# A prefix log-sum-exp scan: six in-place tile buffers, a straight-line TensorE program and a reordered last turn

## The chip, the cores and the metric

The kernel runs on one core of a Trainium2 chip. The metric is device time in microseconds (us), from the start to the end of one execution; the profile's span is a little shorter, since it runs from the first to the last recorded instruction. The core has five engines with their own instruction streams (TensorE or PE, VectorE or DVE, ScalarE or ACT, GpSimd or POOL, SyncE or SP), which meet only at semaphores, and 16 DMA engines that move data between the large memory (HBM) and the on-chip memory (SBUF). In this kernel SP issues all loads and ACT all stores.

## What is computed

```python
B, S, D = 8, 4096, 2048            # x is float32
out[:, 0, :] = x[:, 0, :]
for t in range(1, S):
    mx = np.maximum(out[:, t-1, :], x[:, t, :])
    out[:, t, :] = mx + np.log(np.exp(out[:, t-1, :] - mx) + np.exp(x[:, t, :] - mx))
```

This is a running log-sum-exp along S: out[t] is the logarithm of the sum of exp(x[0..t]), for each batch and each of the 2048 columns. The kernel computes it as Exp, prefix sum, Ln.

## The kernel before

Each batch's 4096 rows are cut into 8 blocks of 512 rows. A tile is one block: 128 partitions with R = 4 consecutive rows each, by D = 2048 columns, 4 MB of float32. There are NT = 64 tiles, n = 0 to 63, and each passes through the same steps, in two halves h of 1024 columns:

- SP loads tile n into an input buffer `ti` (L113 to L125). There are NI = 4 of them.
- ACT takes Exp in place (`exp`, L133).
- DVE adds the four rows within each partition, one running sum of three additions for each half (`local`, L248).
- PE multiplies each partition's last row by a strict triangle of ones (`triangle`, L224), so that every partition gets the sum of all partitions ahead of it. This goes on top of what `carry` (L213) left in the same PSUM bank for the tile before: the running total up to there.
- DVE adds that to all four rows (`join`, L257). After it, `carry` of this tile may read the joined last row for the next tile. At a batch's last block there is no carry, only a semaphore step.
- ACT takes Ln (`ln`, L140) from `ti` into one of NO = 2 output buffers `to`, and issues the store from it (L165).

A column half's semaphore chain is: exps, chain, sums, ahead, joined, carried, logs. ACT's order is written out: Exp of both halves of tile n, Ln of both halves of tile n - 1, the store of n - 1. So a tile's Ln comes behind the Exp of the next tile, and that waits for the next tile's load. The Ln's first half also waits until the store that last used its output buffer has landed (`take(act, stored[n % NO], 16)`, L139). When both Ln are done ACT raises `freed` (L164), for which SP waits before it loads into that input buffer again (L123).

All engines run loops: SP and ACT one turn per four tiles, DVE the same, PE one turn per batch of eight tiles (L233). ACT's last four tiles stand behind its loop. There the Ln is in place, in `ti`, and the store goes out from `ti` (L177). The last turn, n = 63, is ordered Ln half 0 of 62, Exp half 0 of 63, Ln half 1 of 62, the whole store of 62, Exp half 1 of 63; then Ln and store of 63, half by half.

Of the kernel before, what the change touches and what calls it, by code (L numbers as in the profile page):

```python
# [9 lines left out]
def kernel(  # L10
# [15 lines left out]

    nc = tc.nc
    f32 = mybir.dt.float32
    ACT = mybir.ActivationFunctionType
    nc.scalar.preload_act_table_set("natural_log_exp_and_others")  # L34

    B, S, D = x.shape
    P = 128
    R = 4
    NBLK = S // (P * R)
    NT = B * NBLK  # L40
    FD = 512
    NI, NO = 4, 2
    HALF = D // 2
    assert NBLK % NI == 0 and NI % NO == 0 and D == 4 * FD

    pool = ctx.enter_context(tc.tile_pool(name="io", bufs=1))
    psum = ctx.enter_context(tc.tile_pool(name="ps", bufs=1, space=bass.MemoryType.PSUM))
    before = pool.tile([P, P], f32, name="before", tag="before")
    last = pool.tile([P, P], f32, name="last", tag="last")
    ti = [pool.tile([P, R, D], f32, name=f"ti{i}", tag=f"ti{i}") for i in range(NI)]  # L50
    to = [pool.tile([P, R, D], f32, name=f"to{i}", tag=f"to{i}") for i in range(NO)]
    ps = [psum.tile([P, D], f32, name=f"ps{i}", tag=f"ps{i}") for i in range(2)]

    x_v = x.rearrange("b (k p r) d -> (b k) p r d", p=P, r=R)
# [2 lines left out]
    def half(h):  # L57
        return slice(h * HALF, (h + 1) * HALF)
# [17 lines left out]
    def take(engine, s, n):  # L76

        event(engine, [(s, n)], [(s, "sem-sub-imm", n)])

    with tc.tile_critical():  # L80
        def sems(name, n):
            return [nc.alloc_semaphore(f"{name}{i}") for i in range(n)]

        ones, shaped, freed, logs, top, final = (
            sems(s, 1)[0] for s in ("ones", "shaped", "freed", "logs", "top", "final")
        )

        loaded, stored = sems("loaded", NI), sems("stored", NO)
        exps, chain, sums, ahead, joined, carried = (
            sems(s, 2) for s in ("exps", "chain", "sums", "ahead", "joined", "carried")  # L90
        )
# [1 line left out]
        with nc.Block() as block:  # L93
# [17 lines left out]
            @block.sync  # L111
            def _(sp):
                def load(src, n):  # L113
                    sp.dma_start(out=ti[n][:], in_=src).then_inc(loaded[n], 16)


                sp.dma_start(out=ti[0][:, 0:2, :], in_=x_v[0][:, 0:2, :]).then_inc(top, 16)
                sp.dma_start(out=ti[0][:, 2:R, :], in_=x_v[0][:, 2:R, :]).then_inc(loaded[0], 16)
                for n in range(1, NI):
                    load(x_v[n], n)  # L120
                with sp.Fori(1, NT // NI) as j:
                    for n in range(NI):
                        sp.wait_ge(freed, n + 1)  # L123
                        load(x_v[bass.ds(j * NI + n, 1)][0], n)
                    take(sp, freed, NI)  # L125

            @block.scalar
            def _(act):
                def exp(n, h, rows=slice(0, R)):
                    t = ti[n % NI]  # L130
                    if h == 0:
                        take(act, loaded[n % NI], 16)
                    act.activation(  # L133
                        t[:, rows, half(h)], t[:, rows, half(h)], ACT.Exp
                    ).then_inc(exps[h], 1)

                def ln(n, h, turn, in_place=False):
                    if h == 0 and not in_place:
                        take(act, stored[n % NO], 16)  # L139
                    act.activation(  # L140
                        (ti[n % NI] if in_place else to[n % NO])[:, :, half(h)],
                        ti[n % NI][:, :, half(h)], ACT.Ln,
                    )._wait_ge(carried[h], turn + 1).then_inc(logs, 1)

                def settle(turns):
                    take(act, carried[0], turns)
                    take(act, carried[1], turns)
                    take(act, logs, 2 * turns)

                for n in range(NO):  # L150
                    act.sem_inc(stored[n], 16)
                take(act, top, 16)
                act.activation(ti[0][:, 0:2, :], ti[0][:, 0:2, :], ACT.Exp)  # L153
                exp(0, 0, slice(2, R))
                exp(0, 1, slice(2, R))
                turns = (NT - 2) // NI
                with act.Fori(0, turns) as j:
                    for n in range(1, NI + 1):
                        exp(n, 0)
                        exp(n, 1)  # L160
                        ln(n - 1, 0, n - 1)
                        ln(n - 1, 1, n - 1)

                        event(act, [(logs, 2 * n)], [(freed, "sem-add-imm", 1)])  # L164
                        act.dma_start(  # L165
                            out=o_v[bass.ds(j * NI + (n - 1), 1)][0], in_=to[(n - 1) % NO][:]
                        ).then_inc(stored[(n - 1) % NO], 16)
                    settle(NI)


                first = turns * NI
                finals = 0

                def store(n, h=None):
                    cols = slice(0, D) if h is None else half(h)
                    act.wait_ge(logs, 2 * (n - first) + (2 if h is None else h + 1))
                    act.dma_start(  # L177
                        out=o_v[n][:, :, cols], in_=ti[n % NI][:, :, cols]
                    ).then_inc(final, 16)
                    return 1  # L180

                for n in range(first + 1, NT):
                    up = n - 1
                    if n < NT - 1:
                        exp(n, 0)
                        exp(n, 1)
                        ln(up, 0, up - first, True)
                        ln(up, 1, up - first, True)
                        finals += store(up)
                    else:  # L190
                        ln(up, 0, up - first, True)
                        exp(n, 0)
                        ln(up, 1, up - first, True)
                        finals += store(up)
                        exp(n, 1)
                for h in range(2):
                    ln(NT - 1, h, NT - 1 - first, True)
                    finals += store(NT - 1, h)
                settle(NT - first)
                for n in range(NO):  # L200
                    take(act, stored[n], 16)
                take(act, final, 16 * finals)

            @block.tensor
            def _(pe):
                def carry(k, h):

                    if k == NBLK - 1:
                        event(pe, [(joined[h], k + 1)], [(carried[h], "sem-add-imm", 1)])
                        return  # L210
                    for c in range(2 * h, 2 * h + 2):
                        sl = slice(c * FD, (c + 1) * FD)
                        m = pe.matmul(  # L213
                            ps[(k + 1) % 2][:, sl], last[:], ti[k % NI][:, R - 1, sl],
                            start=True, stop=False, skip_group_check=True,
                        )
                        if c == 2 * h:
                            m._wait_ge(joined[h], k + 1)
                    m.then_inc(carried[h], 1)

                def triangle(k, h):
                    for c in range(2 * h, 2 * h + 2):
                        sl = slice(c * FD, (c + 1) * FD)
                        m = pe.matmul(  # L224
                            ps[k % 2][:, sl], before[:], ti[k % NI][:, R - 1, sl],
                            start=k == 0, stop=True, skip_group_check=True,
                        )
                        if c == 2 * h:
                            m._wait_ge(sums[h], k + 1)
                    m.then_inc(ahead[h], 1)  # L230

                pe.wait_ge(shaped, 2)
                with pe.Fori(0, B):  # L233
                    for k in range(NBLK):
                        for h in range(2):
                            triangle(k, h)
                        for h in range(2):
                            carry(k, h)
                    for h in range(2):
                        take(pe, sums[h], NBLK)  # L240
                        take(pe, joined[h], NBLK)

            @block.vector
            def _(dve):
# [14 lines left out]
                        ps[n % 2][:, half(h)].unsqueeze(1).to_broadcast([P, R, HALF]),  # L259
                    )._wait_ge(ahead[h], n + 1).then_inc(joined[h], 1)  # L260

                with dve.Fori(0, NT // NI):
                    for n in range(NI):
                        for h in range(2):
                            local(n, h)
                        for h in range(2):
                            join(n, h)
                    for h in range(2):
                        take(dve, exps[h], NI)
                        take(dve, chain[h], (R - 2) * NI)  # L270
                        take(dve, ahead[h], NI)


# [28 lines left out]
```

The softmax here doesn't subtract the row's maximum and nothing guards it: scores larger than these inputs give would overflow.

## Time and profile before

| | |
|---|---|
| time, median of 5 runs | 1254.31 us (1254.03 to 1257.6) |
| profiled execution | 1254.35 us, span 1252.6 us |
| moved | 268.44 MB read, 268.44 MB written, mean 429 GB/s |
| loads, 4096 KB each | x63, median 33.9 us from issue to landing |
| stores from `to`, 4096 KB each | x60, median 31.4 us |
| stores from `ti` in the last turns | x3 of 4096 KB, median 22.4 us; x2 of 2048 KB, median 7.4 us |
| Exp, one half (L133) | mean 3582 ns, x128 |
| Ln, one half (L140) | mean 3609 ns into `to`, x120; mean 3606 ns in place, x8 |
| row additions (L248), join (L257) | mean 1224 ns, x384; mean 4417 ns, x128 |
| matmuls (L224, L213) | x512 and x448, and as many weight loads |

How to read it: a load or store is far longer from issue to landing than its data needs on the wire, because loads and stores wait behind each other in two queues, one for SP's and one for ACT's. The page gives for each of 40 equal slices of the span the mean busy share of the 16 DMA engines in tenths and the GB/s. Each transfer is split over all 16 DMA engines and counts as landed when the last of them is done. The trace records those 16 completions one by one, and each DMA packet with its queue, start, duration and size. A window view sums the busy time of the engines, the DMA share and the rate for chosen stretches of time, counted from the span's start.

### The profile page before, as it was taken

The page shows a single profiled execution, that of the slowest core. Times are in us where ns is not written, and L with a number is a line of the kernel's source. Part 1 is how long each engine was busy: PE and PEld are TensorE (multiplying, and loading weights), DVE is VectorE, ACT ScalarE, POOL GpSimd, SP SyncE. Part 2 cuts the span into 40 slices and gives each one's busy share as a digit, 9 for nine tenths or more (in the row PEclk, how much of TensorE's full clock was granted, in tenths as well). Part 3 has the DMA queues.
Part 4 walks back from the last instruction along what each step waited for, and adds up shares of the span by engine and source line. Part 5 has one row for each costly group of instructions (what it writes and reads, how often), then busy time and mean ns, then how long its engine had stood idle before and what let it go on. Part 6 is the DMA issues. An engine that isn't in the chain of part 4 may idle for free. (4 is left out here: it accounts for less than half of the span.)

```text
span 1252.6 us, 3677 instructions
## 1 busy us (share of the span) xinstructions
PE 644.1 (51%) x960; PEld 212.4 (17%) x960; DVE 1022.9 (82%) x512; ACT 913.2 (73%) x258; POOL 1.1 (0%) x8
## 2 busy tenths in 40 slices
PE   2556355463554646546455554455645555346552
PEld 0121011121111211112112111111111211111110
DVE  4999788797887877878778788787887878878784
ACT  5886776777767668677686776867768668676884
POOL 0000000000000000000000000000000000000000
PEclk9988677876878867788687786877868877688785
DMA  9999999999999999999999999999999999999997
GB/s 402 419 435 435 430 431 432 431 434 435 435 435 431 430 432 432 433 435 435 435 432 429 433 431 434 434 435 435 432 431 431 431 434 435 434 435 433 429 433 300
DMA packets 19490, 536.90 MB, mean 429 GB/s; under 512 B 2080, under 2 KB 2080, under 8 KB 3104
## 3 DMA queue, kind: packets, MB, share of 16 engines
q1 hardware_dynamic: 9360, 268.44, 49.8%
q10 hardware_dynamic: 10128, 268.44, 49.7%
q8 instruction: 1, 0.02, 0.0%
q14 instruction: 1, 0.01, 0.0%
HBM read 268.44 MB, written 268.44 MB: 429 GB/s over the span
## 5 line engine op out<-in xcount | busy, mean ns | idle before, releaser
L248 DVE TENSOR_TENSOR ti<-ti 128x1024 f32<-128x1024 f32 x384 | 464.7, 1224 | 207.7 <-ACT ti L133 198.9
L140 ACT ACTIVATE to<-ti 128x4096 f32<-128x4096 f32 x120 | 427.6, 3609 | 248.6 <-ACTq L62 244.8
L257 DVE TENSOR_TENSOR ti<-ti,ps 128x4096 f32<-128x4096 f32 x128 | 560.1, 4417 | 9.0 <-PE ps L224 8.7
L224 PE MATMUL ps<-ti,before 128*128 128x512 f32 x512 | 374.7, 882 | 355.1 <-DVE ti L248 354.6
L133 ACT ACTIVATE ti<-ti 128x4096 f32<-128x4096 f32 (+1 forms) x128 | 452.6, 3582 | 59.8 <-ACTq L62 59.4
L213 PE MATMUL ps<-ti,last 128*128 128x512 f32 x448 | 269.6, 732 | 235.5 <-DVE ti L257 235.5
L224 PEld LDWEIGHTS ps<-ti,before 128*128 128x128 f32 x512 | 127.0, 275 | 618.2 <-DVE ti L248 512.9
L213 PEld LDWEIGHTS ps<-ti,last 128*128 128x128 f32 x448 | 85.4, 211 | 402.6 <-DVE ti L257 337.5
L140 ACT ACTIVATE ti<-ti 128x4096 f32<-128x4096 f32 x8 | 28.7, 3606 | 14.5 <-PEq L62 8.9
L153 ACT ACTIVATE ti<-ti 128x4096 f32<-128x4096 f32 x1 | 3.6, 3616 | 6.4 <-ACTq L62 6.4
L34 ACT ACT_TABLE_LOAD x1 | 1.3, 1283 | 0.8 <-PEq L286 0.8
L101 POOL TENSOR_SCALAR_AFFINE_SELECT before<-before 128x128 f32<-128x128 f32 x1 | 0.3, 294 | 0.1
L106 POOL TENSOR_SCALAR_AFFINE_SELECT last<-last 128x128 f32<-128x128 f32 x1 | 0.3, 294 | 0.0
L97 POOL MEMSET before<- 128x128 f32 x1 | 0.2, 205 | 0.5 <-SPq L80 0.5
L98 POOL MEMSET last<- 128x128 f32 x1 | 0.2, 205 | 0.0
L286 POOL MEMSET const-bfloat16-1.0<- 128x1 bf16 x1 | 0.1, 102 | 0.0
L286 POOL MEMSET const-uint8-127<- 128x1 uint8 x1 | 0.1, 102 | 0.0
L286 POOL MEMSET const-float32-0.0<- 128x1 f32 x1 | 0.1, 99 | 0.3 <-issue 0.3
L286 POOL MEMSET const-float32-1.0<- 128x1 f32 x1 | 0.1, 99 | 0.0
## 6 DMA issues: line engine op xcount, KB each, us to landing
ti<-in_x_dram SPq DMA_DIRECT2D x63, 4096.0 KB, 33.9
out_dram<-to ACTq DMA_DIRECT2D x60, 4096.0 KB, 31.4
out_dram<-ti ACTq DMA_DIRECT2D x3, 4096.0 KB, 22.4
ti<-in_x_dram SPq DMA_DIRECT2D x2, 2048.0 KB, 9.6
out_dram<-ti ACTq DMA_DIRECT2D x2, 2048.0 KB, 7.4
```

The lines of the kernel that those rows point to most:

```text
L34: nc.scalar.preload_act_table_set("natural_log_exp_and_others")
L97: g.memset(before[:], 1.0).then_inc(ones, 1)
L101: g.affine_select(out=before[:], in_=before[:], compare_op=mybir.AluOpType.is_ge, fill=0.0, base=-1, pattern=[[1, P]], channel_multiplier= ...
L106: g.affine_select(out=last[:], in_=last[:], compare_op=mybir.AluOpType.is_ge, fill=0.0, base=-(P - 1), pattern=[[0, P]], channel_multiplier=1,
L133: act.activation(t[:, rows, half(h)], t[:, rows, half(h)], ACT.Exp).then_inc(exps[h], 1)
L140: act.activation((ti[n % NI] if in_place else to[n % NO])[:, :, half(h)], ti[n % NI][:, :, half(h)], ACT.Ln,)._wait_ge(carried[h], turn + ...
L153: act.activation(ti[0][:, 0:2, :], ti[0][:, 0:2, :], ACT.Exp)
L213: m = pe.matmul(ps[(k + 1) % 2][:, sl], last[:], ti[k % NI][:, R - 1, sl], start=True, stop=False, skip_group_check=True,)
L224: m = pe.matmul(ps[k % 2][:, sl], before[:], ti[k % NI][:, R - 1, sl], start=k == 0, stop=True, skip_group_check=True,)
L248: a = dve.tensor_add(t[:, r, half(h)], t[:, r - 1, half(h)], t[:, r, half(h)])
L257: dve.tensor_add(t[:, :, half(h)], t[:, :, half(h)], ps[n % 2][:, half(h)].unsqueeze(1).to_broadcast([P, R, HALF]),)._wait_ge(ahead[h], n ...
L286: nc = _bacc.Bacc("TRN2", target_bir_lowering=False, num_devices=1)
```

## The change

- The two output buffers go; there are six buffers `ti`, and Ln is in place for all tiles. Load, Exp, sums, Ln and store of a tile use the same buffer.
- SP waits before a new load for the landing of the store from that buffer (one `stored` semaphore per buffer) instead of for the Ln. The semaphore `freed`, the ScalarE step that raised it and the Ln's wait for an output buffer go. SP also takes the last landings at the end, instead of ACT.
- The loops of SP, ACT and DVE have six tiles per turn, with the remaining four tiles behind them.
- PE has no loop: all 64 tiles are written out, and its semaphores `sums` and `joined` count up to 64.
- The last turn is ordered Exp half 0 of 63, Ln half 0 of 62, store of that half, Exp half 1 of 63, Ln half 1 of 62, store of that half; then Ln and store of 63 by halves, as before.

```diff
-    NI, NO = 4, 2
+    NI = 6
-    to = [pool.tile([P, R, D], f32, name=f"to{i}", tag=f"to{i}") for i in range(NO)]
...
-                with sp.Fori(1, NT // NI) as j:
+                turns = (NT - NI) // NI
+                with sp.Fori(1, turns + 1) as j:
                     for n in range(NI):
-                        sp.wait_ge(freed, n + 1)
+                        take(sp, stored[n], 16)
                         load(x_v[bass.ds(j * NI + n, 1)][0], n)
-                    take(sp, freed, NI)
+                for n in range((turns + 1) * NI, NT):
+                    take(sp, stored[n % NI], 16)
+                    load(x_v[n], n % NI)
+                for n in range(NT - NI, NT):
+                    take(sp, stored[n % NI], 32 if n >= NT - 2 else 16)
...
-                def ln(n, h, turn, in_place=False):
-                    if h == 0 and not in_place:
-                        take(act, stored[n % NO], 16)
+                def ln(n, h, turn):
+                    t = ti[n % NI]
                     act.activation(
-                        (ti[n % NI] if in_place else to[n % NO])[:, :, half(h)],
-                        ti[n % NI][:, :, half(h)], ACT.Ln,
+                        t[:, :, half(h)], t[:, :, half(h)], ACT.Ln
                     )._wait_ge(carried[h], turn + 1).then_inc(logs, 1)
+
+                def store(n, dst, turn, h=None):
+                    cols = slice(0, D) if h is None else half(h)
+                    act.wait_ge(logs, 2 * turn + (2 if h is None else h + 1))
+                    act.dma_start(
+                        out=dst[:, :, cols], in_=ti[n % NI][:, :, cols]
+                    ).then_inc(stored[n % NI], 16)
...
-                        event(act, [(logs, 2 * n)], [(freed, "sem-add-imm", 1)])
-                        act.dma_start(
-                            out=o_v[bass.ds(j * NI + (n - 1), 1)][0], in_=to[(n - 1) % NO][:]
-                        ).then_inc(stored[(n - 1) % NO], 16)
+                        store(n - 1, o_v[bass.ds(j * NI + (n - 1), 1)][0], n - 1)
...
                 for n in range(first + 1, NT):
-                    up = n - 1
+                    up, turn = n - 1, n - 1 - first
+                    exp(n, 0)
                     if n < NT - 1:
-                        exp(n, 0)
                         exp(n, 1)
-                        ln(up, 0, up - first, True)
-                        ln(up, 1, up - first, True)
-                        finals += store(up)
-                    else:
-                        ln(up, 0, up - first, True)
-                        exp(n, 0)
-                        ln(up, 1, up - first, True)
-                        finals += store(up)
+                    ln(up, 0, turn)
+                    if n == NT - 1:
+                        store(up, o_v[up], turn, 0)
                         exp(n, 1)
+                    ln(up, 1, turn)
+                    store(up, o_v[up], turn, 1 if n == NT - 1 else None)
...
-                with pe.Fori(0, B):
-                    for k in range(NBLK):
-                        for h in range(2):
-                            triangle(k, h)
-                        for h in range(2):
-                            carry(k, h)
+                for n in range(NT):
                     for h in range(2):
-                        take(pe, sums[h], NBLK)
-                        take(pe, joined[h], NBLK)
+                        triangle(n, h)
+                    for h in range(2):
+                        carry(n, h)
+                for h in range(2):
+                    take(pe, sums[h], NT)
+                    take(pe, joined[h], NT)
...
-                with dve.Fori(0, NT // NI):
-                    for n in range(NI):
+                def turn(tiles):
+                    for n in range(tiles):
...
+                with dve.Fori(0, NT // NI):
+                    turn(NI)
+                turn(NT % NI)
```

More of the change, by code (lines that the diff above doesn't have):

```diff
@@ L41 @@
     FD = 512
-    NI, NO = 4, 2
+    NI = 6
     HALF = D // 2
-    assert NBLK % NI == 0 and NI % NO == 0 and D == 4 * FD
+    assert NI % 2 == 0 and NBLK % 2 == 0 and D == 4 * FD
     pool = ctx.enter_context(tc.tile_pool(name="io", bufs=1))
@@ L82, in sems @@
             return [nc.alloc_semaphore(f"{name}{i}") for i in range(n)]
-        ones, shaped, freed, logs, top, final = (
-            sems(s, 1)[0] for s in ("ones", "shaped", "freed", "logs", "top", "final")
+        ones, shaped, logs, top = (
+            sems(s, 1)[0] for s in ("ones", "shaped", "logs", "top")
         )
-        loaded, stored = sems("loaded", NI), sems("stored", NO)
+        loaded, stored = sems("loaded", NI), sems("stored", NI)
         exps, chain, sums, ahead, joined, carried = (
@@ L148, in settle @@
                     take(act, logs, 2 * turns)
-                for n in range(NO):
-                    act.sem_inc(stored[n], 16)
                 take(act, top, 16)
@@ L162, in _ @@
                         ln(n - 1, 1, n - 1)
-                        event(act, [(logs, 2 * n)], [(freed, "sem-add-imm", 1)])
-                        act.dma_start(
-                            out=o_v[bass.ds(j * NI + (n - 1), 1)][0], in_=to[(n - 1) % NO][:]
-                        ).then_inc(stored[(n - 1) % NO], 16)
+                        store(n - 1, o_v[bass.ds(j * NI + (n - 1), 1)][0], n - 1)
                     settle(NI)
                 first = turns * NI
-                finals = 0
@@ L174, in store @@
[L174 to L180, printed above, removed]
                 for n in range(first + 1, NT):
-                    up = n - 1
+                    up, turn = n - 1, n - 1 - first
@@ L195, in _ @@
+                    if n == NT - 1:
+                        store(up, o_v[up], turn, 0)
                         exp(n, 1)
+                    ln(up, 1, turn)
+                    store(up, o_v[up], turn, 1 if n == NT - 1 else None)
                 for h in range(2):
-                    ln(NT - 1, h, NT - 1 - first, True)
-                    finals += store(NT - 1, h)
+                    ln(NT - 1, h, NT - 1 - first)
+                    store(NT - 1, o_v[NT - 1], NT - 1 - first, h)
                 settle(NT - first)
-                for n in range(NO):
-                    take(act, stored[n], 16)
@@ L202, in _, with carry @@
-                take(act, final, 16 * finals)
             @block.tensor
             def _(pe):
-                def carry(k, h):
-                    if k == NBLK - 1:
-                        event(pe, [(joined[h], k + 1)], [(carried[h], "sem-add-imm", 1)])
+                def carry(n, h):
+                    if n % NBLK == NBLK - 1:
+                        event(pe, [(joined[h], n + 1)], [(carried[h], "sem-add-imm", 1)])
                         return
@@ L213, in carry @@
                         m = pe.matmul(
-                            ps[(k + 1) % 2][:, sl], last[:], ti[k % NI][:, R - 1, sl],
+                            ps[(n + 1) % 2][:, sl], last[:], ti[n % NI][:, R - 1, sl],
                             start=True, stop=False, skip_group_check=True,
@@ L217, in carry, with triangle @@
                         if c == 2 * h:
-                            m._wait_ge(joined[h], k + 1)
+                            m._wait_ge(joined[h], n + 1)
                     m.then_inc(carried[h], 1)
-                def triangle(k, h):
+                def triangle(n, h):
                     for c in range(2 * h, 2 * h + 2):
@@ L224, in triangle @@
                         m = pe.matmul(
-                            ps[k % 2][:, sl], before[:], ti[k % NI][:, R - 1, sl],
-                            start=k == 0, stop=True, skip_group_check=True,
+                            ps[n % 2][:, sl], before[:], ti[n % NI][:, R - 1, sl],
+                            start=n % NBLK == 0, stop=True, skip_group_check=True,
                         )
                         if c == 2 * h:
-                            m._wait_ge(sums[h], k + 1)
+                            m._wait_ge(sums[h], n + 1)
                     m.then_inc(ahead[h], 1)
                 pe.wait_ge(shaped, 2)
-                with pe.Fori(0, B):
-                    for k in range(NBLK):
-                        for h in range(2):
-                            triangle(k, h)
-                        for h in range(2):
-                            carry(k, h)
-                    for h in range(2):
-                        take(pe, sums[h], NBLK)
-                        take(pe, joined[h], NBLK)
+                for n in range(NT):
+                    for h in range(2):
+                        triangle(n, h)
[4 more added lines that the diff above has]
+                    take(pe, joined[h], NT)
             @block.vector
@@ L268, in _ @@
                     for h in range(2):
-                        take(dve, exps[h], NI)
-                        take(dve, chain[h], (R - 2) * NI)
-                        take(dve, ahead[h], NI)
+                        take(dve, exps[h], tiles)
+                        take(dve, chain[h], (R - 2) * tiles)
+                        take(dve, ahead[h], tiles)
+                with dve.Fori(0, NT // NI):
+                    turn(NI)
+                turn(NT % NI)
 _INS = ['x']
```

## The prediction

> **What bounds the kernel now.** I read the DMA rows of the page first. The kernel moves 268.44 MB in and 268.44 MB out.
>
> ```profile
> PE 644.1 (51%) x960; PEld 212.4 (17%) x960; DVE 1022.9 (82%) x512; ACT 913.2 (73%) x258; POOL 1.1 (0%) x8
> ...
> DMA  9999999999999999999999999999999999999997
> GB/s 402 419 435 435 430 431 432 431 434 435 435 435 431 430 432 432 433 435 435 435 432 429 433 431 434 434 435 435 432 431 431 431 434 435 434 435 433 429 433 300
> ```
>
> Every slice but the last has all 16 DMA engines busy, and no compute engine is above 82%. Then the waits:
>
> ```profile
> ACT to L140 <- ACTq L62: 244.8, 57, 5.6
> ```
>
> This Ln wait, 4.3 us for each of 57 tiles, is ScalarE idle under a full DMA. So time can be won or lost only where a DMA engine is idle, or gets other work. The stage view of the end:
>
> ```profile
> 1205.70:1211.20 5.50, 3.15 (x7) 1.17 (x8) 5.50 (x2) 1.24 (x1) 0.00 (x0) 0.99 1.01 435
> 1211.20:1223.00 11.80, 5.07 (x6) 1.17 (x4) 6.17 (x4) 10.47 (x3) 0.00 (x0) 0.64 1.02 442
> 1223.00:1234.10 11.10, 6.86 (x8) 2.35 (x8) 7.24 (x5) 3.77 (x2) 0.00 (x0) 0.50 0.90 387
> 1234.10:1239.20 5.10, 0.70 (x1) 0.00 (x0) 5.10 (x2) 3.62 (x1) 0.00 (x0) 0.83 0.05 19
> 1239.20:1240.30 1.10, 0.00 (x0) 0.00 (x0) 0.43 (x1) 0.55 (x1) 0.00 (x0) 0.50 0.00 0
> 1240.30:1251.20 10.90, 0.00 (x0) 0.00 (x0) 0.00 (x0) 3.07 (x1) 0.00 (x0) 0.50 0.97 385
> ```
>
> The last two columns are DMA share and GB/s. From 1234.1 to 1239.2 the rate is 19 GB/s, 97 KB in all: three packets of 32 KB. One engine is finishing tile 62's store alone; from 1239.2 to 1240.3 nothing moves.
>
> The landing records show this engine directly: a transfer completes in 16 increments, one for each DMA engine, each with its time. Load 63 lands from 1205.7 to 1211.1. Fourteen engines finish within 0.9 us of the first, one 1.63 us after it, one 5.4 us. Following these two back through all transfers:
> - The 5.4 us engine ("slow") falls behind evenly, 0.09 us in each 19.36 us that a tile takes.
> - The 1.63 us engine ("fetch") keeps time until 107 us, then is suddenly later and stays so. There the queue table's instruction packet went:
>
> ```profile
> q1 hardware_dynamic: 9360, 268.44, 49.8%
> q10 hardware_dynamic: 10128, 268.44, 49.7%
> q8 instruction: 1, 0.02, 0.0%
> ```
>
> The packet records give q8's packet 16,384 bytes and 936 ns from 106.87. On that engine the next packet but one starts at 109.40, where the 1,210 ns rhythm before it pointed to 108.08: 1.32 us lost for one fetch.
>
> The end's compute chain:
>
> ```profile
> 1239.07 0.62 ACTq L177 DMA_DIRECT2D out_dram<-ti  x1
> 1239.75 3.62 ACT L140 ACTIVATE ti<-ti 128x4096 f32<-128x4096 f32 x1 [0.71 <-PEq L62]
> 1243.40 0.54 ACTq L177 DMA_DIRECT2D out_dram<-ti  x1
> ```
>
> Tile 63's half stores are issued at 1239.07 and 1243.40 and land 7.0 and 7.8 us later, the last at 1251.2. The span ends 1.4 us after that, and the execution's 1254.35 is 1.75 more; the median of the runs, 1254.31, is the same within 0.04.
>
> **What the Trainium skill says.** "DMA: Bandwidth & Descriptors", § Where 436 GB/s comes from, puts the ceiling of one core at 435 GB/s; the trace's best slices agree (435). Its § Latency and other measured facts says that two of the 16 engines are usually slower; one here is. Its § Queues, rings and completion order says that each DMA engine serves its own ring of each queue, round robin by packet; the records agree, load and store packets alternating. "Runtime: NRT & Kernel Launch", § Instruction fetch mechanics, says that a sequencer streams its program through its own DMA queue in blocks of 16 KiB, 256 instructions, "mostly hidden". The 16,384-byte packet agrees in size; hidden from the sequencer it is, from a saturated DMA engine it isn't.
>
> **The change, part by part.**
>
> *Six buffers in place.* The same 24 MB is now one pool. A buffer is held from its load's issue to its store's landing. Tiles pass every 19.36 us, so six give 6 x 19.36 = 116 us per buffer. Needed: load and store at half the bandwidth each (2 x 19.4), and between them a wait for the next tile's load, its two Exp and this tile's two Ln (19.4 + 4 x 3.6 = 34): 73 us. The 43 left stand as queued transfers. Neither queue runs dry; if that cover were gone, each missing us would count once per six tiles. The Ln's wait on an output buffer goes (244.8 us of idle ScalarE): what is late next is the load, so nothing comes of it. SP now waits for a store's landing instead of the Ln's end; behind it stand only later loads, which the bigger pool covers. At the start six loads are queued instead of four, but store 0 and load 4 already follow load 3 without a gap (load 3's first landing 43.98, then 16 packets to load 4's at 63.35): 0. VectorE's and ScalarE's new loop lengths: same instructions, hidden: 0.
>
> *The last turn.* The 14 quick engines finish store 61 at 1223.87 and have no idle time before it. Then come tiles 62 and 63, now four half stores. Back to back one takes 5.12 us (first landings of the two in before, 1245.87 and 1250.99): 20.5, so 1244.35. Is the data there? Tile 63's chain from its load's landing, with the rows' durations: Exp 3.7, Ln of 62 with its issue 4.0, Exp 3.6, three adds 3.7, joins 4.4 and 4.4, Ln 3.6, so half stores at about 23 and 28 us. A quick engine has 39 us of stores left when it finishes load 63, less what the latest engine's lag delays the chain. Any engine that is itself late has its full 39 and no gap. So the idle 6 us of the quick engines goes. But the slow engine idled only 1.4 us (1239.1 to about 1240.5): it would end near 1244.35 + 5.5 = 1249.9, against 1251.2. That is the gain, 1.3 us, if nothing else comes.
>
> *Straight-line TensorE program.* 960 weight loads, 960 matmuls and about 20 more are now about 1,940 instructions, each passed once. The loop before has a 1/8 of them and was fetched once at its first pass. The fetch at 107 us came after about 185 instructions. One more each 256 gives 185, 441, 697, 953, 1209, 1465, 1721: seven fetches instead of one (six or eight if the last block is counted otherwise). The records of before show one per queue, so not whether all come through one DMA engine. Bounds: 0, where each finds another engine; 7 x 1.32 = 9.25 where all go to one. I take one, because a ring belongs to a queue and an engine. Then the fetch engine ends at 1244.35 + 0.31 (its place before 107 us) + 9.25 = 1253.9. A TensorE stall while a block arrives would be hidden: its work has the 43 us above.
>
> *The sum.* Last landing 1253.9 instead of 1251.2, +2.7 us: 1254.35 + 2.7 = 1257.0.
>
> **The rivals.**
> 1. *The fetches cost nothing on the path* (spread over engines). The slow engine ends last, 1249.9: -1.3, 1253.0, not slower. For: "mostly hidden"; a later 8 KB fetch, near 1183 us, fell on a third engine, 0.68 us late. Against: that one is of another queue (q14), and the first one was not hidden from its engine. It decides at four fetches or fewer on one engine: 0.31 + 4 x 1.32 = 5.6, the slow engine's lag.
> 2. *And the slow engine isn't slow any more*, its drift being an effect of the loops. All 16 end at about 1244.9: -6.3, 1248.0, faster. For: the drift has no named cause in the trace. Against: it is even through all loop turns.
> 3. *The fetches fall on the slow engine.* 5.5 + 9.25 = 14.8 behind: last landing 1259.1, +7.9, 1262.3. Against: in before it was another one.
> 4. *In-place buffers starve the loads.* By the 43 us above, excluded unless compute stalls by that much.
>
> **How the numbers follow.** 0.2% is 2.5 us, about what a measurement here can tell from no change; the edge is 1256.8. Forecast 0.56, with its own range 1255.6 (six fetches) to 1258.5 (eight); rival 1 0.22; rival 2 0.11; rival 3 0.09; rival 4 0.02. The forecast's centre lies just beyond the edge, so it gives 0.34 to slower and 0.22 to no change. Faster: rival 2 and a little of rival 1, 0.13. Same 0.42. Slower 0.45. The range takes in rival 1 and the forecast, 1252.0 to 1260.0.
>
> **What would show it.** q8 with seven packets, about 0.11 MB; one DMA engine losing 1.3 us about every 155 us; load 63's landing spread near 9.6 us instead of 5.4; no zero-rate stretch on that engine in the last turn; the rate falling to one engine's for the last several us; ScalarE's Ln waiting for no store. One q8 packet only, a spread of 5.4, or a q8 landing on changing engines would make it wrong; so would a row of slices under 430 GB/s in the middle, which would mean starved queues.

## The result and the profile after

The changed kernel takes 1250.88 us (median), the kernel before 1254.32: a ratio of 0.9967, 95% interval 0.996 to 0.9974. The forecast was 1257.0, slower; it is faster by 3.4 us. The profiled execution took 1250.61 us, span 1248.9. All ratios compare mean times and leave out slow executions, over 1.5% above the fastest of their kernel: here one of the changed kernel's 27 (1276.74), below two of e6's six.

The page of the changed kernel, the rows that were read first before:

```profile
span 1248.9 us, 3456 instructions
...
PE 653.6 (52%) x960; PEld 216.0 (17%) x960; DVE 1023.3 (82%) x512; ACT 907.2 (73%) x258; POOL 1.1 (0%) x8
...
DMA  9999999999999999999999999999999999999998
GB/s 403 420 436 428 431 435 436 430 433 432 435 435 429 435 430 436 436 428 435 431 436 435 429 436 431 435 436 429 436 430 436 436 428 436 431 435 435 429 436 357
...
q1 hardware_dynamic: 9360, 268.44, 49.9%
q10 hardware_dynamic: 11040, 268.44, 49.9%
q8 instruction: 7, 0.11, 0.0%
```

Little changed in the middle: full DMA, and compute times within 2% of those before. The last slice moved 357 GB/s instead of 300. And q8 has seven packets: the count of instruction fetches came as forecast. The end in stages (us, then busy time of PE, PEld, DVE, ACT and POOL, the TensorE clock, DMA share and GB/s):

```profile
1223.00:1234.10 11.10, 3.78 (x4) 1.17 (x4) 9.27 (x3) 5.66 (x3) 0.00 (x0) 0.50 0.96 397
1234.10:1239.20 5.10, 0.00 (x0) 0.00 (x0) 0.00 (x0) 1.91 (x1) 0.00 (x0) 0.50 1.03 422
1239.20:1240.30 1.10, 0.00 (x0) 0.00 (x0) 0.00 (x0) 0.00 (x0) 0.00 (x0) 0.50 1.02 417
1240.30:1251.20 10.90, 0.00 (x0) 0.00 (x0) 0.00 (x0) 0.00 (x0) 0.00 (x0) 0.51 0.39 162
```

Where before moved 19 and 0 GB/s, from 1234.1 to 1240.3, all DMA engines now work, and the low rate has moved to the very end, where single engines finish. Who makes them late is in the landing records, read as in the prediction: 16 completions for each transfer. Here they are for four loads, worked out from the trace: first the time at which the first engine is done, then the lag of each of the 16 behind it, in us, sorted:

```
 139.5  0.0 0.0 0.0 0.0 0.1 0.1 0.2 0.5 0.5 0.5 0.5 0.5 0.5 0.6 0.6 2.1
 488.0  0.0 0.0 0.0 0.0 0.1 0.1 0.5 0.5 0.5 0.5 0.5 0.5 1.6 1.8 2.0 2.0
 836.6  0.0 0.0 0.0 0.0 0.1 0.1 0.5 0.5 0.5 0.5 1.8 1.8 1.9 1.9 2.0 2.6
1185.1  0.0 0.0 0.1 0.5 0.5 0.5 0.5 1.0 1.4 1.5 1.8 1.8 1.8 1.9 2.0 3.8
```

Each fetch moves one more engine by about 1.3 us, and never the same one: at the end seven engines stand between 1.4 and 2.0, none at 9.6. The last number of the last row, 3.8, is the slow engine, whose lag grows evenly from load to load; no fetch hit it. It lands the last store at 1247.5, again 3.8 us behind the first. The forecast had the fetch engine at 1253.9.

The waits show a second difference. In the view of who waited for whom (in total, times, longest), the wait ahead of Exp before and now:

```profile
ACT ti L133 <- ACTq L62: 59.4, 63, 6.0
...
ACT ti L136 <- ACTq L59: 304.1, 63, 6.0
```

Before, ScalarE waited 244.8 us ahead of Ln and 59.4 ahead of Exp, together 304.2. Now it waits 304.1 ahead of Exp and for no store ahead of Ln. The idle time hasn't shrunk, it stands at another place in each tile.

### The profile page after: what moved, and what is told of

Same layout as the page of the kernel before. It is cut to its first block, busy times and chain, and to the rows that moved or that the text cites. A ratio compares the mean times of both kernels' runs of the same rounds, so it can differ in the third digit from the quotient of the medians.

```text
span 1248.9 us, 3456 instructions
## 1 busy us (share of the span) xinstructions
PE 653.6 (52%) x960; PEld 216.0 (17%) x960; DVE 1023.3 (82%) x512; ACT 907.2 (73%) x258; POOL 1.1 (0%) x8
## 5 line engine op out<-in xcount | busy, mean ns | idle before, releaser
L136 ACT ACTIVATE ti<-ti 128x4096 f32<-128x4096 f32 (+1 forms) x128 | 452.6, 3582 | 310.1 <-ACTq L59 304.1
L208 PE MATMUL ps<-ti,before 128*128 128x512 f32 x512 | 379.9, 894 | 339.5 <-DVE ti L232 338.9
L142 ACT ACTIVATE ti<-ti 128x4096 f32<-128x4096 f32 x128 | 455.4, 3602 | 11.5 <-PE ps L197 6.0
L197 PE MATMUL ps<-ti,last 128*128 128x512 f32 x448 | 273.9, 743 | 234.3 <-DVE ti L241 234.3
L159 ACT ACTIVATE ti<-ti 128x4096 f32<-128x4096 f32 x1 | 3.6, 3616 | 6.5 <-ACTq L59 6.5
## 6 DMA issues: line engine op xcount, KB each, us to landing
ti<-in_x_dram SPq DMA_DIRECT2D x63, 4096.0 KB, 38.4
out_dram<-ti ACTq DMA_DIRECT2D x62, 4096.0 KB, 43.9
```

Of the source, the lines that this page charges most:

```text
L136: act.activation(t[:, rows, half(h)], t[:, rows, half(h)], ACT.Exp).then_inc(exps[h], 1)
L142: act.activation(t[:, :, half(h)], t[:, :, half(h)], ACT.Ln)._wait_ge(carried[h], turn + 1).then_inc(logs, 1)
L197: m = pe.matmul(ps[(n + 1) % 2][:, sl], last[:], ti[n % NI][:, R - 1, sl], start=True, stop=False, skip_group_check=True,)
L208: m = pe.matmul(ps[n % 2][:, sl], before[:], ti[n % NI][:, R - 1, sl], start=n % NBLK == 0, stop=True, skip_group_check=True,)
```

## Experiments

Ratios are to the kernel before, from runs on the same chip, with the 95% interval in brackets. Since they compare means, one long execution moves them more than it moves the median.

### The kernel before, again (e1)

No edit.

> The kernel before, unchanged, for the lag of the slow DMA engine. If the smaller lag in the changed kernel (3.9 us behind the first engine at the end, 5.5 in the profile before) is chance from run to run, this profile gives some other value, anywhere from 3 to 6 us. If the lag belongs to the kernel, it is again 5.3 to 5.7 us at load 63. Time 1253.5 to 1255 either way.

Measured: 1253.88 us, ratio 1.0003 (0.9994 to 1.0012). In its profile the slow engine is 4.4 us behind at the store of tile 61, the last one ahead of the gap; in the profile on record it was 5.5. So this lag isn't a fixed property of the kernel, and the 5.5 that the prediction carried over is the highest of the six profiles in which Ln waits for a store.

### The last turn alone (e2)

```diff
                 for n in range(first + 1, NT):
                     up = n - 1
+                    exp(n, 0)
                     if n < NT - 1:
-                        exp(n, 0)
                         exp(n, 1)
...
+                    ln(up, 0, up - first, True)
+                    if n == NT - 1:
+                        finals += store(up, 0)
+                        exp(n, 1)
+                    ln(up, 1, up - first, True)
+                    finals += store(up, 1 if n == NT - 1 else None)
```

> The kernel before with only the last turn reordered and tile 62 stored by halves. If the last turn is the whole gain: 3.4 us faster, 1250.9. If it is only the slow engine's idle time (2.2 us lost between the stores of 62 and 63 in the profile before) and the rest comes from the smaller lag of that engine in the changed kernel: 2.0 us faster, about 1252.3.

Measured: 1251.89 us, 0.9983 (0.9977 to 0.999): 2.2 us less than before. The stage in which before moved 19 GB/s:

```profile
1234.10:1239.20 5.10, 0.00 (x0) 0.00 (x0) 0.00 (x0) 2.83 (x1) 0.00 (x0) 0.50 1.03 413
```

The gap is gone: on its own, the new order is enough to close it.

### The straight-line TensorE program alone (e3)

In the kernel before, the loop of L233 becomes `for n in range(NT)`, as in the change.

> The kernel before with only the TensorE program written out. Seven instruction packets. If each falls on another DMA engine: no change, 1254.3 within 0.5 us, and the landing spread of load 63 stays that of the slow engine. If they piled up on one engine, as the prediction had it: its lag 9.6 us at load 63, and since this kernel's last turn waits for that landing, 4 us slower, 1258.5. If leaving out the loop is what makes the slow engine less slow: lag 3.8 instead of 5.4, and 1.6 us faster, 1252.7.

Measured: 1254.11 us, 1.0004 (0.9996 to 1.0011), seven q8 packets, the slow engine 4.5 us behind at tile 61's store. Within that interval, about 1 us either way, seven fetches cost nothing and leaving out the loop brings nothing. This is the term on which the forecast's sign stood.

### The change without its last turn (e4)

The changed kernel with Ln half 0 of 62 ahead of Exp half 0 of 63 again, and tile 62 stored whole.

> The changed kernel with the last turn in the order of before and tile 62 stored whole. If the last turn is the whole gain: back at 1254.3. If the gain is split between it and the smaller lag: 2.0 us slower than the changed kernel, about 1252.9.

Measured: 1250.75 us, 0.9978 (0.9967 to 0.9989). Neither expectation: without the new last turn the changed kernel is as fast as with it. Its end on ScalarE (start, duration, then what it is and the idle time ahead of it):

```profile
1208.13 3.62 ACT L142 ACTIVATE ti<-ti 128x4096 f32<-128x4096 f32 x1 [3.53 <-PE ps L200]
1211.65 3.60 ACT L136 ACTIVATE ti<-ti 128x4096 f32<-128x4096 f32 x1
...
1234.67 0.63 ACTq L149 DMA_DIRECT2D out_dram<-ti  x1
```

The order is that of before, but all of it is 4.4 us earlier: the Ln at 1208.13 stood at 1212.53, and the store of tile 63's first half was issued at 1239.07. The slow engine finishes tile 62 at 1237.8, and now its next data is there. (One execution of 1255.11 among seven raises the ratio.) So something in the six in-place buffers and their waits brings the tail forward, a second way to close the same gap.

### Both, with two separate output buffers (e5)

The kernel before with e2's last turn and e3's TensorE program.

> The kernel before with the new last turn and the straight-line TensorE program, but with the two separate output buffers. The last turn alone gave 1251.9, the changed kernel gives 1250.9. If the missing 1 us comes with the six in-place buffers: 1251.9 again. If it comes with the missing TensorE loop: 1250.9.

Measured: 1251.55 us, 0.9972 (0.9961 to 0.9982). The interval overlaps those of the changed kernel and of e2. The median lies nearer to e2's, but the median of before beside it was 0.5 us higher too (1254.58 against 1254.05). It doesn't decide.

### Which wait it is (e11, e12)

e11 takes e4 and puts back one thing: Ln of tile n waits for the store of tile n - 2. SP counts the landings in a semaphore of its own (`take` waits for a count and subtracts it).

```diff
                         take(sp, stored[n], 16)
+                        sp.sem_inc(landed, 1)
...
+                act.sem_inc(landed, 2)
...
+                        take(act, landed, 1)
                         ln(n - 1, 0, n - 1)
```

> The changed kernel with the last turn of before (1250.75 without the following) and one wait put back: the first Ln of tile n waits, as before, until the store of tile n - 2 has landed. If this wait is what made the kernel before late in its last turn, by holding back the Exp of the next tile: Exp of tile 63 late again by about 4 us, the gap between the stores of 62 and 63 is back, and the time is 1253 to 1254. If the in-place buffers close the gap in another way: 1250.8.

Measured: 1253.94 us, 0.9991 (0.9977 to 1.0006): the whole gain is gone. The gap is back, at the same 19 GB/s as before:

```profile
1234.10:1239.20 5.10, 0.23 (x1) 0.00 (x0) 5.10 (x2) 3.62 (x1) 0.00 (x0) 0.82 0.05 19
```

and so is the late Ln of tile 62:

```profile
1212.30 3.62 ACT L144 ACTIVATE ti<-ti 128x4096 f32<-128x4096 f32 x1 [5.98 <-PE ps L204]
```

e12 is the same program with `act.sem_inc(landed, 4)`, so that the wait asks for a store that has long landed; the two counts left over are taken at the end.

> The kernel with the wait put back (1253.94), with the same instructions, but the wait asks for the store of tile n - 4 instead of n - 2, so that it is always met. If holding the Ln back is what costs: back at 1250.8, no gap between the last stores, and the slow engine 3.9 to 4.3 us behind at the store of tile 61, as in the four profiles without that wait (4.4 to 5.5 in the six with it). If the 120 more semaphore instructions themselves slow that engine: its lag stays at 4.8, and about 1251.5.

Measured: 1250.94 us, 0.997 (0.9957 to 0.9983). The instructions are the same but for the two counts at the end, nothing waits, and the gain is there: 3.0 us between the medians of e11 and e12, on two chips whose medians for the kernel before agree (1254.22 and 1254.28). Tile 62's Ln starts 2.8 us earlier than in e11:

```profile
1209.49 3.62 ACT L144 ACTIVATE ti<-ti 128x4096 f32<-128x4096 f32 x1 [3.36 <-PE ps L205]
```

This profile is of the longest of e12's nine executions (1254.86), with the slow engine 8.3 us behind, so it doesn't decide between the two lags that were expected. But the gap can be told apart from the lag. Here, worked out from the landings, are the lag of the last engine at tile 61's store, the time at which that store has landed, the last landing of all, and what lies between the two (us):

```
before           5.5   1229.4   1251.2   21.8
e11              4.9   1228.7   1251.0   22.3
e12              8.3   1232.0   1251.6   19.6
e4               4.1   1228.0   1247.6   19.6
e2               4.8   1228.7   1248.5   19.7
changed kernel   3.9   1227.7   1247.5   19.8
```

With the gap the last two tiles' stores take 21.8 to 24.0 us (before, e1, e3, e11), without it 19.6 to 19.8 (the other four above, and e5, e7, e8, e9). So e12's long execution is one whose slow engine came late to tile 61. An engine that finishes tile 62 only at 1241.7, as there, would have found its next data in e11's order too (issued at 1238.84), so the gain is shown by e12's other eight executions, 1250.80 to 1251.34 us against 1252.68 to 1255.25 in e11, and by the earlier Ln.

How the wait works is seen a few tiles ahead of the end. The timeline of before, at tile 61 (the Ln is that of tile 59, the Exp that of 61):

```profile
1169.89 7.13 ACT L140 ACTIVATE to<-ti 128x4096 f32<-128x4096 f32 x2 [4.50 <-ACTq L62]
1177.26 0.35 ACTq L165 DMA_DIRECT2D out_dram<-to  x1
1178.14 7.12 ACT L133 ACTIVATE ti<-ti 128x4096 f32<-128x4096 f32 x2 [1.12 <-ACTq L62]
```

and of the changed kernel, tile 61's Exp and tile 60's Ln:

```profile
1169.52 7.12 ACT L136 ACTIVATE ti<-ti 128x4096 f32<-128x4096 f32 x2 [5.29 <-ACTq L59]
1176.55 7.11 ACT L142 ACTIVATE ti<-ti 128x4096 f32<-128x4096 f32 x2
1183.69 0.35 ACTq L149 DMA_DIRECT2D out_dram<-ti  x1
```

Before, load 61 had landed at 1172.2, but ScalarE was held in front of Ln until tile 57's store had landed, and came to the Exp only at 1178.14, 5.9 us after its data. In the changed kernel the load lands at 1169.4 and the Exp starts 0.1 us later. In the middle of the run these 6 us cost nothing, since the DMA queues are full. At the end nothing refills them: VectorE runs back to back from tile 61 on (16.2 us a tile), and 4.4 us of the lateness are left at tile 62's Ln.

### The other parts (e7, e8)

e7: the changed kernel with tile 62 stored whole after both its Ln.

> The changed kernel with tile 62 stored whole after both its Ln, instead of by halves. If the slow engine's continuous work sets the end: two half stores took 9.9 us on it, a whole one 9.7, so 0.2 us faster, 1250.7. If the early half store is needed to keep that engine busy: slower by the idle time it would fill, 1 us or more.

Measured: 1250.79 us, 0.9961 (0.9946 to 0.9977). The half stores are neither needed nor dear. e8 puts one line ahead of loads 4 and 5:

```diff
                 for n in range(1, NI):
+                    if n >= 4:
+                        sp.wait_ge(logs, 2 * (n - 3))
                     load(x_v[n], n)
```

> The changed kernel, but loads 4 and 5 are issued only when Ln of tiles 0 and 1 are done, as in the kernel before, instead of at the start. If the six loads queued up front are what makes the DMA engines start more evenly (the spread of the first landings after 40 us is 0.4 us in the changed kernel, 0.5 to 1.9 us with four loads): about 0.9 us slower, 1251.8. If not: 1250.9.

Measured: 1251.01 us, 0.9963 (0.995 to 0.9977). The longer queue at the start brings nothing.

### How far fetches can be driven (e6, e9, e10)

e6 adds `for _ in range(128): pe.wait_ge(shaped, 2)` to each tile's TensorE program.

> The changed kernel with 128 more TensorE instructions per tile, waits on a semaphore that is already raised, so that about 39 blocks are fetched instead of 7. If the fetches go round the 16 DMA engines and each costs its engine 1.32 us, the slow engine gets two or three of them: 2.6 to 4.0 us slower than the changed kernel, 1253.5 to 1254.9. If a fetch costs nothing when DMA engines are full[...]: 1250.9. If all went through one engine: 39 x 1.32 = 51 us, about 1298.

Measured: 1286.06 us, with six executions between 1278.98 and 1302.66, and 1.0217 (1.0182 to 1.0252). There are 23 q8 packets, not 39, since the waits went two to an instruction: 7,552 instructions against 3,456. The profile is of one of the two longest executions (1301.68), so only these counts are taken from it. The loss over the changed kernel, about 31 us by the two ratios, is some ten times what the price of a fetch gives, so either a fetch has another cost or the waits do. e9 adds instructions that are no waits: every matmul is cut into four of 128 columns.

```diff
-                    for c in range(2 * h, 2 * h + 2):
-                        sl = slice(c * FD, (c + 1) * FD)
+                    for c in range(8 * h, 8 * h + 8):
+                        sl = slice(c * FD // 4, (c + 1) * FD // 4)
```

What the pieces leave in PSUM isn't what the whole matmuls leave, so the prefix sums are not those of the reference; transfers and waits are as described, and VectorE and ScalarE are as busy as in the changed kernel (1023.2 and 907.2 us).

> The changed kernel with every matmul cut into four of 128 columns: the same sums, about 7,700 TensorE instructions instead of 1,940, about 30 fetches instead of 7. If fetches go round the DMA engines at 1.32 us each, every engine gets about two: 2.6 us slower than the changed kernel, 1253.5. If instead the 35 us of the kernel with many waits came from the fetches in some other way, they come again here: 1280 or more. If the slow engine gets none: 1250.9.

Measured: 1257.63 us, 1.0018 (1.0004 to 1.0032), some 6.4 us more than the changed kernel by the two ratios. The queue row:

```profile
q8 instruction: 30, 0.49, 0.1%
```

Thirty fetches, and no 31 us: what e6 lost wasn't the fetches. The lags of the DMA engines in the profile of e9 (an execution of 1255.89 us), for three loads:

```
 720.6  0.0 0.1 0.4 0.7 0.7 0.9 1.1 2.7 2.8 3.0 3.4 3.5 3.9 4.2 5.7 6.5
 953.0  0.0 0.1 0.4 0.7 0.7 0.8 1.1 3.5 4.1 4.2 4.2 4.7 5.2 5.5 5.6 8.1
1146.6  0.0 0.1 0.4 0.7 0.7 0.9 1.1 4.0 4.7 4.8 5.5 5.6 5.6 6.6 7.0 9.5
```

Seven engines don't move at all between 720 and 1147 us. The last one, the slow engine, rises evenly, 0.27 us per 38.7 us, without a step. The eight between them rise in steps of 1.3 us: from the first row to the last, with eleven fetches between, together from 29.2 us behind to 43.8, 1.33 us for each fetch. So the fetches go round eight of the 16 engines, and the slow one isn't among them in this run. That it drifts twice as fast here as in the changed kernel (9.3 us behind at tile 61's store, not 3.9) is what costs the time of this execution, since from there to the last landing both take 19.8 us. Why it drifts faster was not found.

e10 puts e6's waits into a small loop, to execute them with few fetches.

> The changed kernel with the same 128 additional waits per tile on TensorE, but in a small loop, so that some 10 to 12 blocks are fetched instead of 23. If executing the waits is what stretched the DMA packets and cost 35 us: 1280 or more again. If the fetches did: about 1251 to 1252.

Measured: 1461.92 us, 1.1649 (1.1601 to 1.1697), ten q8 packets. The view of waits says why it can't answer the question:

```profile
PEld ps L208 <- issue: 774.9, 445, 17.9
...
DVE ti L244 <- PE ps L208: 401.8, 64, 7.2
```

TensorE's own instruction stream is now the bound (774.9 us in which its weight loads waited for nothing but issue), VectorE waits for it, and the time is that of another kernel.

## Why the prediction was wrong

- **DMA as the bound, the idle gap at 1234 to 1240 us, 1.32 us for a fetch, seven fetches:** all held. Seven packets came, and e9 confirms the price (1.33).
- **"I take one, because a ring belongs to a queue and an engine":** this step failed, and with it the sign. The fetches fall on different DMA engines, so each engine loses 1.3 us once, below the slow engine's lag, and the path loses nothing (e3: 1.0004). Of the two bounds written down, 0 and 9.25 us, the lower was right. That is rival 1, at 1253.0; one packet in the trace before could not tell the two apart. The Trainium skill's "DMA: Bandwidth & Descriptors", § Queues, rings and completion order, gives a queue one ring on each of 16 engines; that a queue's fetches stay on one of them was an inference of mine, not its statement. Its "Runtime: NRT & Kernel Launch", § Instruction fetch mechanics, has the fetch "mostly hidden", and for seven of them e3 agrees.
- **"The Ln's wait on an output buffer goes ... so nothing comes of it":** this failed too, the other way. It is worth 3.0 us with the old last turn (e11 against e12), nearly all of the gain. The working looked at the share of idle time, which indeed doesn't change, and not at where in a tile it stands. Moved from in front of Ln to in front of Exp, it lets each tile start when its load lands, and in the last tiles that is 4.4 us.
- **The last turn, -1.3 us:** right in direction and too small when it stands alone (e2: -2.2), but wrong in the sum: the removed wait closes the same gap, so on top of it the new order brings nothing (e4 against the changed kernel). Two edits that fill one gap were costed as if only one did.
- **Sizes:** rival 1 was still 2.1 us too slow. Its quick engines end at 1243.7 instead of 1244.35, since a half store that follows another takes 4.97 us there, not 5.12 as the pair of before; why it takes less, no run shows. Its slow engine is 3.8 us behind instead of 5.5. Together that is 2.3 us at the last landing.
- **Loads, start, loop lengths, buffers held longer: 0.** Held: e8 shows it for the start. From issue to landing loads now take 38.4 us and stores of whole tiles 43.9 (medians); less the 2 x 19.4 of their own, 43.5 us are spent queued, where 43 were worked out as cover.

What stays open is the lag of the slow engine. The medians of e2 and e5 are 1.0 and 0.7 us above that of the changed kernel (1.3 and 0.4 when each is set against before beside it). In their profiles the last two tiles take no longer (19.7 us each); the difference is there when tile 61's store has landed, at 1228.7 and 1228.5 us against 1227.7. The lag at that store is 4.4 to 5.5 us in the six profiles with the Ln's wait (before, e1, e2, e3, e5, e11), 3.9 to 4.2 in four without it (after, e4, e7, e8), and 8.3 in the long execution of e12. The single profiles of e3 (4.5) and e8 (4.2) give no sign that the TensorE loop or the early loads cause it, and two executions of the same kernel differ as much (5.5 before, 4.4 in e1).

No version beats the changed kernel beyond its interval: e4, e7 and e8 are the same. The plainest of them is e4, which needs no reordered last turn.

## What to carry to other kernels

In this kernel, idle time of an engine off the bound cost nothing in the middle of the run. But ask where it stands in the engine's order: a wait ahead of one tile's last step also held back the next tile, whose data had landed, while a wait for that data itself holds back nothing else. At the end, where no queue covers it, that lateness is paid once. When two edits fill the same gap, price each with the other in place. And when a cost falls on one of many parallel engines, the trace must show on which, more than once, before it is summed on one.

## What was not expected of the hardware

- A 16 KiB instruction fetch takes 1.32 us out of one DMA engine under full load; successive fetches of TensorE's program used seven different engines in the changed kernel, and 28 of them, until 1147 us, went round eight in e9.
- 4,096 additional instructions that wait on raised semaphores (64 per tile) cost about 2.5% over the changed kernel (e6, with a wide spread), where 5,760 more weight loads and matmuls cost about 0.5% (e9, both by their ratios). What in the waits costs the time was not found.
- One DMA engine falls behind the others all through every run that keeps the DMA full: by 3.9 to 5.5 us at tile 61's store in ten profiles, 8.3 in e12's and 9.3 in e9's, and differently in two executions of one kernel. In e10, which leaves DMA time idle, the last engine is 0.2 us behind there.
